# Seven block products for eight in half of the first feed-forward product, with one weight sum of a step made by an adding DMA

## The chip, the cores and the metric

The kernel runs on one core of one Trainium2 chip. The time is device microseconds of one execution. The profile shows the engines PE (matrix products; PEld is its weight load), DVE (vector), ACT (scalar functions), POOL and SP (here the engine that issues most DMAs), and the DMA queues.

## The reference

One layer of a residual block in float32: 256 positions, 2048 channels, a feed-forward width of 8192. Two mixing branches (retention and latent attention) are gated, added and multiplied by w_out; then comes the feed-forward part, which is what the change touches.

```python
    merged = jax.nn.sigmoid(g_ret) * y_ret + jax.nn.sigmoid(g_mla) * y_mla
    return merged @ w_out
...
        h = h + _mixer(u, positions, w_in[l], ret_norm_g[l], w_ret_o[l], q_a_norm_g[l],
                       w_q_b[l], kv_a_norm_g[l], w_kv_b[l], w_mla_o[l], w_out[l])
        z = _rmsnorm(h, norm_mlp_g[l]) @ w_up[l]
        h = h + jnp.square(jax.nn.relu(z)) @ w_down[l]
    return _rmsnorm(h, norm_f_g)
```

w_up is 2048 x 8192 and w_down 8192 x 2048, 64 MB each in float32.

## The kernel before

**Precision.** Every float32 operand x is split in two: a high part `hi`, the value rounded to the PE's reduced 32-bit format by a cast on ACT (L151), and a low part `lo = x - hi`, a subtraction on DVE (L152). A product is then three: hi x hi, lo x hi and hi x lo.

**Weights.** `weights` (L146 to L153) loads a block of 128 x 1024 elements (512 KB) with a DMA from SP's queue (L148) into one of five `raw` buffers, and splits it into one of four `hi` and one of four `lo` buffers. A load waits until the split of five blocks earlier has freed its buffer; a split waits until PE has done with the block four earlier.

**w_out stage.** Its products have the form in which the activation is the stationary operand (128 x 128) and 512 weight columns move (L199, L200, L202). For each of four column blocks, the sums are added to the residual `hn` (L778) and their squares summed (L779). `mlp_turn` transposes a finished block of `hn` by PE products with a unit matrix (L764) and splits it with the norm's gain (L219, L220) into `hT`, which holds the feed-forward input transposed, high and low part side by side. The norm's factor is left out here and put in at the end (`rh2`, squared), which the squared ReLU permits.

**First feed-forward product ("up").** It is done in 64 units of 128 columns of w_up (`t_unit`). Here the weights are stationary. A unit has two weight blocks. In `t_pass1` (L159) sixteen matmuls multiply the high parts of the weights by high and low part of `hT` in one go (512 columns: 256 positions twice); in `t_pass2` (L163) sixteen more multiply the low parts by `hT`'s high part (256 columns). Then `joined` adds the two halves of the accumulator: ACT copies one half out of PSUM (L206) and DVE adds (L207). One DVE operation (L800) squares the ReLU into `hid`, which stays on the chip: 64 tiles of 128 x 256. The first two units are started with the first half of the channels while `mlp_turn(3)` still prepares the last quarter of `hT`.

**Second product ("down").** For each of the 64 tiles of `hid`, ACT and DVE split it (L216, L217) and 24 matmuls (L814 to L816) multiply it with two w_down blocks into eight PSUM accumulators (`dn`), which take all eight banks. After the last tile the residual is added, the final norm computed and the output stored.

**Buffers.** PSUM has eight banks of 128 x 512: four from the pool that `mmps` takes, four from the pool of `atps`. `big` gives out six large SBUF slots of 16 KB per partition, which tensors take in turn as earlier ones die.

**Order.** Each engine works through its own queue in order. The order in a queue is not that of the program text: at build time a scheduler with a simulated timeline places the instructions of the whole program, so weight splits stand well ahead of the matmuls that use them. DMA loads stand in SP's queue, one behind the other; a load whose buffer is not free holds those behind it.

Of the kernel before, what the change touches and what calls it, by code (L numbers as in the profile page):

```python
# [19 lines left out]
P = 128  # L20
# [9 lines left out]
FT = DFF // P  # L30
EPS = 1e-6
# [57 lines left out]
def block_kernel(ctx: ExitStack, tc: tile.TileContext, A):  # L89
# [43 lines left out]
    def mmps(name):  # L133
        return pmm.tile([P, 512], F32, tag="mm", name=name)
# [68 lines left out]

    def join(out, ps):
        t = sm.tile([P, S], F32, tag="join", bufs=2, name="join")
        SC.copy(t, ps[:, S:])  # L206
        V.tensor_tensor(out=out, in0=ps[:, :S], in1=t, op=ALU.add)  # L207
# [25 lines left out]
    cold = cp.tile([P, 512], BF16, name="cold")  # L233
# [5 lines left out]
    rctx = ExitStack()  # L239
    rope_pool = rctx.enter_context(tc.tile_pool(name="rope", bufs=2))  # L240
# [109 lines left out]
    rxb = cp.tile([P, S], F32, name="rxb")  # L350
# [4 lines left out]
    def table(j):  # L355
        ang, kk = angs[j]
        sgn = vec[:, V_INV + 2 + j : V_INV + 3 + j]
        own = ip if j == 0 else cp
        cos = own.tile([P, S], F32, name=f"cos{j}")
        sin = own.tile([P, S], F32, name=f"sin{j}")  # L360
# [158 lines left out]
    with ExitStack() as mctx:  # L519
        cc = big("cc", F32R, shape=(P, 2 * LT, 2, S))  # L520
        kpe = cp.tile([P, S], F32, name="kpe")
# [245 lines left out]
    hp = ctx.enter_context(tc.tile_pool(name="hp", bufs=1))  # L767
    ssh = cp.tile([P, 2, 4], F32, name="ssh")
# [16 lines left out]
    up = [mmps(f"z{i}") for i in range(2)]  # L785
    for i in range(2):
        t_half(up[i], A["w_up"][i], hT, 0)
        if i == 0:
            mlp_turn(3)
    hid = [big(f"hid{i}") for i in range(3)]  # L790
    hid.append(hp.tile([P, KT, S], F32, name="hid3"))
    for i in range(FT):
        if i < 2:
            pz = up[i]
            t_half(pz, A["w_up"][i], hT, 1)
        else:
            pz = mmps(f"z{i}")
            t_unit(pz, A["w_up"][i], hT)
        z = joined(pz)
        V.scalar_tensor_tensor(hid[i // KT][:, i % KT], in0=z, scalar=0.0, in1=z, op0=ALU.max, op1=ALU.mult)  # L800
# [18 lines left out]
    for i in range(FT):  # L819
        dh = hp.tile([P, S], F32R, tag="dh", bufs=3, name=f"dh{i}")  # L820
        dl = hp.tile([P, S], F32R, tag="dl", bufs=3, name=f"dl{i}")
        split(dh, dl, hid[i // KT][:, i % KT])
        ws = []
        for half in range(2):
            w = weights(A["w_down"][i][:, half * 1024 : (half + 1) * 1024], [P, 1024])
            ws.append(w)
            if i < FT - LAST:
                for t in range(2):
                    for c in (2 * half, 2 * half + 1):
                        down(i, t, c, w, (dh, dl))  # L830
        if i >= FT - LAST:
            tail.append((i, ws, (dh, dl)))
# [7 lines left out]
    def finish(t, c, lo, hi, n):  # L840
# [3 lines left out]
        junk = hp.tile([P, 512], F32, tag="junk", bufs=2, name=f"junk{t}{n}")  # L844
# [101 lines left out]
```

## Time and profile before

| | |
|---|---|
| median of 3 runs | 1631.94 us (1631.42 to 1632.12) |
| the profiled execution | 1632.22 us, its span in the profile 1630.4 us |
| PE, DVE, ACT, POOL busy | 1614.9, 996.2, 809.7, 49.5 us |
| granted TensorE clock, mean | 0.998 |
| DMA moved | 304.46 MB, mean 187 GB/s |
| first z matmul, first dn matmul | 915.47 us, 1272.66 us from the span's start |
| weight loads of w_up: 128 of 512 KB | 4.2 us from issue to landing (median) |
| loads of 256 KB (w_mla_o; con) | 2.6 us; 13.4 us |
| stores of 256 KB (out) | 2.5 us |

A group's line in the profile reads: line, engine, operation, output<-inputs, shapes, count | busy us, mean ns of one | idle us of the engine just before, and what ended it. A window's row reads: start:end, length, then busy us and (instructions) of PE, PEld, DVE, ACT and POOL, then the granted PE clock as a share of full speed, the busy share of the DMA engines, and GB/s. A line of the timeline reads: start, duration, engine, line, operation, and how many instructions were run together.

### The profile page before, as it was taken

Reading aid. Unit: us, or ns where it says so; the run is one execution under the profiler, and the core shown is the slowest. Engines: PE = TensorE matmul, PEld = TensorE weight load, DVE = VectorE, ACT = ScalarE, POOL = GpSimd, SP = SyncE. Lnnn points to the kernel's source line nnn. Section 1 sums busy time; section 2 is a strip of 40 time slices with the busy share of each in tenths; the row PEclk is TensorE's granted clock in tenths of the full one; section 3 lists DMA queues with packets and bytes.
Section 4 is the critical chain, followed back from the end, with each engine's and each line's share of the span. In section 5 each row is a group of like instructions: output and inputs, shape, how many; then the busy total and the mean of one; then the engine's idle time right before and its main releaser. Section 6 shows DMA issues by size and latency. Waiting matters only on the chain.

```text
span 1630.4 us, 23041 instructions
## 1 busy us (share of the span) xinstructions
PE 1614.9 (99%) x8782; PEld 1398.8 (86%) x8782; DVE 996.2 (61%) x1491; ACT 809.7 (50%) x1249; POOL 49.5 (3%) x62
## 2 busy tenths in 40 slices
PE   8999999999999999999999999999999999999997
PEld 6888888888889889888888888888888888888886
DVE  7974588655556658666765555555555555555555
ACT  6544555544445556765545544444444444444444
POOL 7100000000000000000000000000000000000001
PEclk9999999999999999999999999999999999999999
DMA  8665544555556554325575555555555655555553
GB/s 306 200 233 193 187 156 166 169 192 186 190 170 203 190 191 146 125 94 176 186 246 187 174 193 188 192 189 186 191 192 184 223 194 192 193 193 195 192 194 112
DMA packets 84480, 304.46 MB, mean 187 GB/s; under 512 B 9360, under 2 KB 9488, under 8 KB 83600
## 3 DMA queue, kind: packets, MB, share of 16 engines
q1 hardware_dynamic: 84368, 302.98, 55.3%
q8 instruction: 69, 1.13, 0.3%
q14 instruction: 43, 0.35, 0.1%
HBM read 300.84 MB, written 2.10 MB: 186 GB/s over the span
## 4 chain that ended last, share of the span: by engine, by line
PE 97%; DVE 1%; issue 0%; DMA 0%; ACT 0%; POOL 0%; SPq 0%; DVEq 0%; POOLq 0%; ACTq 0%
PE z L159 14%; PE z L163 8%; PE dn L816 7%; PE dn L814 7%; PE dn L815 7%; PE rg L159 4%; PE yr L159 4%; PE gr L159 4%; PE gm L159 4%; PE mo L159 4%; PE qk L159 2%; PE gr L163 2%; PE yr L163 2%; PE gm L163 2%; PE rg L163 2%; PE mo L163 2%
## 5 line engine op out<-in xcount | busy, mean ns | idle before, releaser
L152 DVE TENSOR_TENSOR lo<-raw,hi 128x1024 fp32r<-128x1024 f32 (+2 forms) x562 | 666.0, 1204 | 521.6 <-ACT hi L151 248.3
L151 ACT CAST hi<-raw 128x1024 fp32r<-128x1024 f32 (+2 forms) x562 | 580.8, 1035 | 536.9 <-PE z L159 135.2
L159 PE MATMUL z<-hT,hi 128*128 128x512 f32 x1024 | 245.5, 391 | 0.0
L159 PEld LDWEIGHTS z<-hT,hi 128*128 128x128 f32 x1024 | 188.0, 188 | 36.1
L815 PE MATMUL dn<-lo,dh 128*128 128x512 f32 x512 | 199.2, 389 | 0.0
L816 PE MATMUL dn<-hi,dl 128*128 128x512 f32 x512 | 199.2, 389 | 0.0
L814 PE MATMUL dn<-hi,dh 128*128 128x512 f32 x512 | 198.9, 389 | 0.0
L163 PEld LDWEIGHTS z<-hT,lo 128*128 128x128 f32 x1024 | 131.6, 191 | 5.1
L163 PE MATMUL z<-hT,lo 128*128 128x256 f32 x1024 | 133.1, 283 | 0.0
L815 PEld LDWEIGHTS dn<-lo,dh 128*128 128x128 f32 x512 | 96.1, 188 | 20.1
L816 PEld LDWEIGHTS dn<-hi,dl 128*128 128x128 f32 x512 | 96.1, 188 | 19.9
L814 PEld LDWEIGHTS dn<-hi,dh 128*128 128x128 f32 x512 | 96.1, 188 | 19.8
L216 ACT CAST dh<-hid 128x256 fp32r<-128x256 f32 x64 | 26.0, 407 | 89.3 <-PE dn L815 89.3
L159 PE MATMUL mo<-my,hi 128*128 128x512 f32 x256 | 65.5, 396 | 0.4 <-DVE val L207 0.4
L159 PE MATMUL rg<-x,hi 128*128 128x512 f32 x256 | 64.0, 395 | 0.0
L159 PE MATMUL yr<-ry,hi 128*128 128x512 f32 x256 | 61.4, 391 | 0.0
L159 PE MATMUL gr<-x,hi 128*128 128x512 f32 x256 | 61.3, 391 | 0.0
L159 PE MATMUL gm<-x,hi 128*128 128x512 f32 x256 | 61.1, 391 | 0.0
L159 PEld LDWEIGHTS gm<-x,hi 128*128 128x128 f32 x256 | 47.0, 188 | 9.1
L159 PEld LDWEIGHTS gr<-x,hi 128*128 128x128 f32 x256 | 47.0, 188 | 9.0
L159 PEld LDWEIGHTS yr<-ry,hi 128*128 128x128 f32 x256 | 46.9, 188 | 9.0
L159 PEld LDWEIGHTS rg<-x,hi 128*128 128x128 f32 x256 | 46.2, 188 | 8.6
(271 smaller groups left out, 2239.1 us busy)
## 6 DMA issues: line engine op xcount, KB each, us to landing
raw<-w_up SPq DMA_DIRECT2D x128, 512.0 KB, 4.2
raw<-w_down SPq DMA_DIRECT2D x128, 512.0 KB, 4.3
raw<-w_rv SPq DMA_DIRECT2D x32, 512.0 KB, 4.5
raw<-w_rg SPq DMA_DIRECT2D x32, 512.0 KB, 4.5
raw<-w_gret SPq DMA_DIRECT2D x32, 512.0 KB, 4.3
raw<-w_ret_o SPq DMA_DIRECT2D x32, 512.0 KB, 4.6
raw<-w_gmla SPq DMA_DIRECT2D x32, 512.0 KB, 4.4
raw<-w_out SPq DMA_DIRECT2D x32, 512.0 KB, 3.7
```

Source lines behind the costliest of these rows:

```text
L151: SC.copy(hi, raw)
L152: V.tensor_tensor(out=lo, in0=raw, in1=hi.bitcast(F32), op=ALU.subtract)
L159: PE.matmul(out, w[0][:, k], x.both(k0 + k), start=start and k == 0, stop=False)
L163: PE.matmul(out[:, :S], w[1][:, k], x.hi(k0 + k), start=False, stop=stop and k == n - 1)
L216: SC.copy(hi, val)
L814: mm(PE.matmul(out, dh[:, ts], hi[:, ws], start=i == 0, stop=False))
L815: mm(PE.matmul(out, dh[:, ts], lo[:, ws], start=False, stop=False))
L816: mm(PE.matmul(out, dl[:, ts], hi[:, ws], start=False, stop=end))
```

## The change

The first 4096 of w_up's 8192 columns are no longer done in units. They are done by Strassen's scheme in the form with seven products: the operand is seen as 2 x 2 blocks, here 128 positions by 128 channels, the weights as 2 x 2 blocks of 128 channels by 512 columns, and seven products of sums of blocks stand for eight products of blocks.

- **Groups and steps.** Four groups `u` of 1024 columns, each of eight steps `j` of 256 channels. A step (`s_step`) does the seven products of one pair of channel blocks, three matmuls of 512 columns each (hi x hi, lo x hi, hi x lo; L271 to L273), into seven accumulators `qs` that live through the whole group, in seven PSUM banks. The operand sum is now the stationary operand and the weights move.
- **Weight sums.** Of the four 128 x 512 weight blocks of a step two are loaded as `ra`, one as `rb` and one into the buffer `f1`. The first sum is made by a DMA from POOL's queue that adds another block (read from DRAM) onto the one that lies in `f1` (L248). The three others are DVE operations (L253 to L255). There are three `f1` buffers in turn and one `f2`. Then the seven weight operands are split as before, four splits with seven 512-column blocks in total.
- **Operand sums.** `Combos` forms the four sums of `hT`'s blocks that are needed and splits them, in four parts: parts 0 and 1 within the w_out stage (L869), parts 2 and 3 among the early units. They use `raw` buffers as scratch.
- **End of a group.** `s_end` forms the four output blocks from the seven accumulators, with one ACT copy and seven DVE operations of 512 columns. The result lies with the positions in the partitions; `turn` transposes it on PE, 16 transposes in four parts for each group, and `square` works on two 128-column tiles at once. The parts are called in the middle of later steps.
- **Units.** The other 4096 columns stay units; three early ones and two late ones frame the mixture of steps and units.
- **hid.** `square` now computes ReLU and square on ACT, in one buffer `hs`, and stores the result to DRAM from ACT's queue. Down reads it back in 32 loads (`hl`, L963) from SP's queue, and starts with the tiles of the units. `hn` is stored to DRAM too (L920) and read back before the end (L939).
- Some constants of earlier stages move to a pool that is released, and w_up's first half is laid out in steps on the host.

```diff
@@ -28,6 +28,11 @@
 CHUNK = 64
 DFF = 8192
 FT = DFF // P
+SU = 4
+SJ = KT // 2
+ST = SU * 1024 // P
+EARLY, LATE = 3, 2
+SSF = 68
 EPS = 1e-6
 QK_SCALE = float(192.0 ** -0.5)
 LOWEST = -3.4e38
@@ -201,6 +206,88 @@
         for k in range(nk):
             PE.matmul(out, x.hi(k0 + k, ts), w[1][:, k], start=False, stop=stop and k == nk - 1)
 
+    PRODUCTS = ((3, 0, 0), (4, 0, 1), (2, 1, 0), (6, 1, 1), (5, 2, 0), (1, 2, 1), (7, 3, 0))
+    count = [0]
+
+    class Combos:
+        FORM = {2: 0, 5: 1, 6: 2, 4: 3}
+        RAW = {1: (1, 0), 3: (0, 1), 7: (1, 1)}
+
+        def __init__(self, name, pair):
+            self.name, self.pair, self.t = name, pair, []
+
+        def make(self, c):
+            if c % 2 == 0:
+                self.t.append(big(f"{self.name}{c // 2}", F32R, (P, KT // 4, 2, 4, P)))
+            x, q = wtile("raw", [P, 2, 2, 2, P]), wtile("raw", [P, 2, 4, P])
+            hi, lo = self.pair.span(4 * c, 4)
+            xs = x.rearrange("p j k t n -> p (j k) (t n)")
+            V.tensor_tensor(out=xs, in0=hi.bitcast(F32), in1=lo.bitcast(F32), op=ALU.add)
+            a11, a12, a21, a22 = (x[:, :, k, t] for t in range(2) for k in range(2))
+            a2, a5, a6, a4 = (q[:, :, f] for f in range(4))
+            V.tensor_tensor(out=a2, in0=a11, in1=a12, op=ALU.subtract)
+            V.tensor_tensor(out=a5, in0=a11, in1=a21, op=ALU.subtract)
+            V.tensor_tensor(out=a6, in0=a2, in1=a21, op=ALU.subtract)
+            V.tensor_tensor(out=a4, in0=a6, in1=a22, op=ALU.add)
+            o = self.t[-1][:, c % 2 * 2 : c % 2 * 2 + 2]
+            split(o[:, :, 0], o[:, :, 1], q)
+
+        def get(self, f, j):
+            if f in self.RAW:
+                k, t = self.RAW[f]
+                ts = slice(t * P, (t + 1) * P)
+                return self.pair.hi(2 * j + k, ts), self.pair.lo(2 * j + k, ts)
+            o = self.t[j // 4][:, j % 4]
+            return o[:, 0, self.FORM[f]], o[:, 1, self.FORM[f]]
+
+    def s_step(qs, src, x, j, between):
+        uid[0] += 1
+        f1, f2 = forms[:, count[0] % 3], forms[:, 3]
+        count[0] += 1
+        nc.sync.dma_start(f1[:, 0], src[:, 3])
+        G.dma_start(f1[:, 0], src[:, 0], accum_op=ALU.add)
+        ra = zp.tile([P, 2, 512], F32, tag="ra", bufs=3, name=f"ra{uid[0]}")
+        rb = zp.tile([P, 1, 512], F32, tag="rb", bufs=3, name=f"rb{uid[0]}")
+        nc.sync.dma_start(ra, src[:, :2])
+        nc.sync.dma_start(rb, src[:, 2:3])
+        V.tensor_tensor(out=f1[:, 1], in0=f1[:, 0], in1=ra[:, 1], op=ALU.add)
+        V.tensor_tensor(out=f2[:, 0], in0=f1[:, 1], in1=ra[:, 0], op=ALU.subtract)
+        V.tensor_tensor(out=f2[:, 1], in0=f1[:, 1], in1=rb[:, 0], op=ALU.add)
+        ws = []
+        for i, r in enumerate((ra, f1, f2, rb)):
+            if i in (1, 2):
+                hi, lo = (
+                    zp.tile([P, 2, 512], F32R, tag=kind, bufs=4, name=f"{kind}{uid[0]}{i}") for kind in ("shi", "slo")
+                )
+            else:
+                hi, lo = (wtile(kind, [P, r.shape[1], 512]) for kind in ("hi", "lo"))
+            split(hi, lo, r)
+            ws.append((hi, lo))
+        for n, (f, i, o) in enumerate(PRODUCTS):
+            if n == 4:
+                between()
+            (ah, al), (hi, lo) = x.get(f, j), ws[i]
+            first, last = j == 0, j == SJ - 1
+            PE.matmul(qs[f], ah, hi[:, o], start=first, stop=False)
+            PE.matmul(qs[f], al, hi[:, o], start=False, stop=False)
+            PE.matmul(qs[f], ah, lo[:, o], start=False, stop=last)
+
+    def s_end(qs, out, tmp):
+        t3, e, f = (tmp[:, i] for i in range(3))
+        c11, c12, c21, c22 = (out[:, t, c] for t in range(2) for c in range(2))
+
+        def tt(o, a, b, op=ALU.add):
+            V.tensor_tensor(out=o, in0=a, in1=b, op=op)
+
+        SC.copy(t3, qs[3])
+        tt(e, qs[6], t3)
+        tt(f, qs[2], e, ALU.subtract)
+        tt(c21, qs[4], f)
+        tt(c11, qs[5], f)
+        tt(e, e, qs[5], ALU.subtract)
+        tt(c12, qs[1], e)
+        tt(c22, qs[7], t3)
+
     def join(out, ps):
         t = sm.tile([P, S], F32, tag="join", bufs=2, name="join")
         SC.copy(t, ps[:, S:])
...
@@ -774,6 +866,8 @@
             n_unit(pss, A["w_out"][4 * c + kq], mg, 4 * kq, 4, kq == 0, kq == 3)
             if kq == 0 and c:
                 mlp_turn(c - 1)
+        if c in (1, 2):
+            hc.make(c - 1)
         for t in range(2):
             V.tensor_tensor(out=hn[:, t, cs], in0=pss[t], in1=hn[:, t, cs], op=ALU.add)
             SC.activation(pss[t], hn[:, t, cs], AF.Square, accum_out=ssh[:, t, c : c + 1])
@@ -782,25 +876,72 @@
     V.tensor_scalar(rh2, rh2, 1.0 / D, EPS, op0=ALU.mult, op1=ALU.add)
     V.reciprocal(rh2, rh2)
 
-    up = [mmps(f"z{i}") for i in range(2)]
-    for i in range(2):
-        t_half(up[i], A["w_up"][i], hT, 0)
+    hid = [hidd.tile([P, 2, S], F32, name=f"hid{i}") for i in range(FT // 2)]
+    zo = big("zo", shape=(P, 2, 4, 512))
+
+    def square(pair, n, val):
+        t = zp.tile([P, 2, S], F32, tag="hs", bufs=1, name=f"hs{pair}{n}")[:, : val.shape[1]]
+        SC.activation(t, val, AF.Relu)
+        SC.activation(t, t, AF.Square)
+        SC.dma_start(hid[pair][:, n : n + val.shape[1]], t)
+
+    def s_units():
+        turns = []
+        for u in range(SU):
+            qs = {f: (mmps if f in (3, 4, 2, 5) else atps)(f"zs{u}{f}") for f in range(1, 8)}
+            for j in range(SJ):
+                s_step(qs, A["w_up_s"][u, j], hc, j, turns.pop(0) if turns and j else lambda: None)
+                yield
+            s_end(qs, zo[:, 0].rearrange("p (t c) n -> p t c n", t=2), zo[:, 1])
+
+            def turn(u, jj):
+                pT = atps(f"zt{u}{jj}")
+                for j in range(2):
+                    kt = 2 * jj + j
+                    for t in range(2):
+                        o = j * S + t * P
+                        src = zo[:, 0, 2 * t + kt // 4, kt % 4 * P : kt % 4 * P + P]
+                        PE.transpose(pT[:, o : o + P], src, ident)
+                square(4 * u + jj, 0, pT.rearrange("p (j n) -> p j n", j=2))
+
+            turns = [lambda u=u, jj=jj: turn(u, jj) for jj in range(4)]
+        for fn in turns:
+            yield
+            fn()
+
+    forms = None
+    steps = s_units()
+    early = [atps(f"z{i}") for i in range(EARLY)]
+    for i, pz in enumerate(early):
+        t_half(pz, A["w_up"][i], hT, 0)
         if i == 0:
             mlp_turn(3)
-    hid = [big(f"hid{i}") for i in range(3)]
-    hid.append(hp.tile([P, KT, S], F32, name="hid3"))
-    for i in range(FT):
-        if i < 2:
-            pz = up[i]
-            t_half(pz, A["w_up"][i], hT, 1)
-        else:
-            pz = mmps(f"z{i}")
-            t_unit(pz, A["w_up"][i], hT)
-        z = joined(pz)
-        V.scalar_tensor_tensor(hid[i // KT][:, i % KT], in0=z, scalar=0.0, in1=z, op0=ALU.max, op1=ALU.mult)
+            keep = hidd.tile([P, 2, D], F32, name="hnkeep")
+            SC.dma_start(keep, hn)
+            hc.make(2)
+            forms = big("forms", shape=(P, 4, 2, 512))
+    for i, pz in enumerate(early):
+        t_half(pz, A["w_up"][i], hT, 1)
+        square((ST + i) // 2, i % 2, joined(pz).unsqueeze(1))
+        if i == 0:
+            hc.make(3)
+    done = 0
+    for i in range(EARLY, FT - ST):
+        while done < SU * SJ and done * (FT - ST - EARLY - LATE) <= (i - EARLY) * SU * SJ:
+            next(steps)
+            done += 1
+        pz = atps(f"z{i}")
+        t_unit(pz, A["w_up"][i], hT)
+        square((ST + i) // 2, i % 2, joined(pz).unsqueeze(1))
+    for _ in steps:
+        pass
+    hn = big("hn2", shape=(P, 2, D))
+    nc.sync.dma_start(hn, keep)
+    zctx.close()
+    jp = ctx.enter_context(tc.tile_pool(name="jp", bufs=1))
 
     pd = [[(mmps if t == 0 else atps)(f"dn{t}{c}") for c in range(4)] for t in range(2)]
-    ssf = cp.tile([P, 2, 68], F32, name="ssf")
+    ssf = cp.tile([P, 2, SSF], F32, name="ssf")
     rf = cp.tile([P, 2], F32, name="rf")
     LAST = 2
 
@@ -816,20 +957,23 @@
         mm(PE.matmul(out, dl[:, ts], hi[:, ws], start=False, stop=end))
 
     tail = []
-    for i in range(FT):
+    for n, i in enumerate((*range(ST, FT), *range(ST))):
+        if n % 2 == 0:
+            hl = hp.tile([P, 2, S], F32, tag="hl", bufs=3, name=f"hl{i}")
+            nc.sync.dma_start(hl, hid[i // 2])
         dh = hp.tile([P, S], F32R, tag="dh", bufs=3, name=f"dh{i}")
         dl = hp.tile([P, S], F32R, tag="dl", bufs=3, name=f"dl{i}")
-        split(dh, dl, hid[i // KT][:, i % KT])
+        split(dh, dl, hl[:, i % 2])
         ws = []
         for half in range(2):
             w = weights(A["w_down"][i][:, half * 1024 : (half + 1) * 1024], [P, 1024])
             ws.append(w)
-            if i < FT - LAST:
+            if n < FT - LAST:
                 for t in range(2):
                     for c in (2 * half, 2 * half + 1):
-                        down(i, t, c, w, (dh, dl))
-        if i >= FT - LAST:
-            tail.append((i, ws, (dh, dl)))
+                        down(n, t, c, w, (dh, dl))
+        if n >= FT - LAST:
+            tail.append((n, ws, (dh, dl)))
     gf = big("gf", shape=(P, D))
     nc.sync.dma_start(gf, A["norm_f_g"].partition_broadcast(P))
     for t in range(2):
...
@@ -883,6 +1027,13 @@
     k, n = w.shape
     u = w.reshape(k // 512, 4, P, n // 512, 512).transpose(3, 0, 2, 1, 4)
     return np.ascontiguousarray(u.reshape(-1, P, 4, 512))
+
+
+def _s_steps(w):
+    k, n = w.shape
+    b = w.reshape(k // 256, 2, P, n // 1024, 2, 512)
+    q = np.stack([b[:, 0, :, :, 1], b[:, 1, :, :, 0], b[:, 1, :, :, 1], b[:, 0, :, :, 0]], axis=3)
+    return np.ascontiguousarray(q.transpose(2, 0, 1, 3, 4))
 
 
 def _cols(v):
...
```

More of the change, by code (lines that the diff above doesn't have):

```diff
@@ L231, in block_kernel @@
     SC.activation(warm, halfpi, AF.Copy)
[L233 removed]
+    rctx = ExitStack()
+    rope_pool = rctx.enter_context(tc.tile_pool(name="rope", bufs=2))
+    cold = rope_pool.tile([P, 512], BF16, tag="cold", bufs=1, name="cold")
     V.memset(cold, 0.0)
@@ L357, in table @@
         sgn = vec[:, V_INV + 2 + j : V_INV + 3 + j]
-        own = ip if j == 0 else cp
-        cos = own.tile([P, S], F32, name=f"cos{j}")
-        sin = own.tile([P, S], F32, name=f"sin{j}")
+        cos, sin = (
+            (ip if j == 0 else rope_pool).tile([P, S], F32, tag=f"{name}{j}", bufs=1, name=f"{name}{j}")
+            for name in ("cos", "sin")
+        )
         tc.keep_in_program_order(SC.activation(sin, ang, AF.Sin, scale=sgn))
@@ L931 @@
         "w_out": _n_units(np.asarray(w_out)[0]),
-        "w_up": _t_units(np.asarray(w_up)[0]),
+        "w_up_s": _s_steps(np.asarray(w_up)[0][:, : SU * 1024]),
+        "w_up": _t_units(np.asarray(w_up)[0][:, SU * 1024 :]),
         "w_down": np.ascontiguousarray(np.asarray(w_down)[0].reshape(FT, P, D)),
```

14 lines of the change are left out of this document (8 added, 6 removed).

## The prediction

> **What bounds the kernel now.** I read the busy shares first, then the chain that ended last, then the table of one stretch for the feed-forward stages, then the stage's instructions in order of time on PE, and last the groups on DVE and ACT.
>
> ```profile
> PE 1614.9 (99%) x8782; PEld 1398.8 (86%) x8782; DVE 996.2 (61%) x1491; ACT 809.7 (50%) x1249; POOL 49.5 (3%) x62
> ...
> PE 97%; DVE 1%; issue 0%; DMA 0%; ACT 0%; POOL 0%; SPq 0%; DVEq 0%; POOLq 0%; ACTq 0%
> ```
>
> PE is busy 99% of the span and 97% of the ending chain. So every matmul removed is time, as long as PE stays fed, and every us of PE idle is time too.
>
> ```profile
> core 0: us, PE busy (x) PEld busy (x) DVE busy (x) ACT busy (x) POOL busy (x), PEclk, DMA share, GB/s
> 915.00:1272.00 357.00, 357.00 (x2054) 315.26 (x2053) 202.05 (x267) 162.52 (x203) 0.00 (x0) 1.00 0.56 189
> 1300.00:1400.00 100.00, 100.00 (x443) 82.81 (x442) 53.01 (x56) 44.72 (x56) 0.00 (x0) 1.00 0.58 194
> ```
>
> The first row is the first feed-forward product: PE never idle, DVE at 202 of 357 us (57%), ACT 46%, POOL at nothing, DMA 56%. The second row gives a price: 443 matmuls of 512 columns in 100 us, 0.2257 us each.
>
> ```profile
> 944.23 3.82 PE L159 MATMUL z<-hT,hi 128*128 128x512 f32 x16
> 947.88 2.08 PE L163 MATMUL z<-hT,lo 128*128 128x256 f32 x16
> 949.79 3.82 PE L159 MATMUL z<-hT,hi 128*128 128x512 f32 x16
> ```
>
> One unit (128 columns of w_up) takes 949.79 - 944.23 = 5.56 us: sixteen 512-column matmuls from 944.23 to 947.88 (0.228 each), sixteen of 256 in 1.91 (0.119). The first z matmul starts at 915.47, the first dn one at 1272.66: 357.2 us over 64 units, 5.58 each.
>
> ```profile
> L152 DVE TENSOR_TENSOR lo<-raw,hi 128x1024 fp32r<-128x1024 f32 x538 | 648.4, 1225 | 500.5 <-ACT hi L151 231.3 <-PE z L163 145.1 <-PE gr L163 36.1
> L207 DVE TENSOR_TENSOR val<-z,join 128x256 f32<-128x256 f32 x64 | 26.7, 417 | 0.0
> L800 DVE SCALAR_TENSOR_TENSOR hid<-val 128x256 f32<-128x256 f32 x64 | 27.1, 424 | 2.1
> L151 ACT CAST hi<-raw 128x1024 fp32r<-128x1024 f32 x538 | 565.1, 1052 | 513.3 <-PE z L159 135.2 <-PE dn L816 99.2 <-PE rv L200 43.2
> ```
>
> DVE and ACT wait for PE to free the weight buffers: slack today. Rows overlap at their ends. Back to back, a 1024-column subtraction takes 1.14 us of DVE, a 512-column one 0.63, a 256-column one 0.34; the cast takes 0.97 of ACT, 0.6 for 512 columns.
>
> **The change, part by part.** Times t count from the first z matmul.
>
> *PE.* 32 units go: 32 x 5.57 = 178.3 us. In come 32 steps of 7 products x 3 matmuls of 512 columns, 672 in all. The w_out stage, which has this form (12 matmuls, 907.30 to 910.03), gives 0.2267 each: 152.3 us, 4.76 a step. The 64 transposes cost 0.067 to 0.09 each (the ht rows); at 0.08, 5.1 us. Net 178.3 - 152.3 - 5.1 = **20.9 us saved**; with 0.2257 and 0.2285 a matmul and the ends for a transpose, 19 to 22.5.
>
> *DVE and ACT.* A step needs on DVE three weight sums (512 columns, 3 x 0.63) and the low parts (3 x 1.14 + 0.63): 5.94 us against PE's 4.76. A kept unit needs 2 x 1.14 + 0.34 = 2.62 against 5.57, since its squaring (L800) moves to ACT. Five units lie at the ends, so 32 steps and 27 units are mixed: per step DVE 5.94 + 0.84 x 2.62 = 8.1, PE 4.76 + 0.84 x 5.57 = 9.4. Over the stage DVE gets 129.6 + 60.5 + 18 (28 block sums) + 84 (units) + 10 (operand sums) = 302 us of about 350, 86% instead of 57%. A step's ACT work is 3 x 0.97 + 0.6 = 3.5, a unit's 1.94 + 0.37 and a relu and a square of some 0.4 each: less than DVE's. So PE stays the bound on average, with 14% of cover where there was 43%. In the first of the four groups I sum DVE to 78 us and PE to 75: there a wait of DVE on ACT is time. Such waits total 3.8 us of 357 in the trace of before; bounds 0 and 8 (10% of 78): **2.5 us**.
>
> *The start.* PE has three early units (11.7 us) before the first products, with two operand sums behind them on DVE. Following DVE's queue with the periods above, it reaches the first weight sum at t = 10.5 and the first operand cast is ready at 12.3; from there DVE leads and PE is latest, by **3.5 us**, around the fourth unit (27.8 if PE were the bound, 31.3 by DVE); bounds 1 and 6. The two operand sums placed in w_out put some 5 us each on DVE and ACT and hold 2 of 5 raw buffers; DVE has over 1 us free per 2.72 us of PE there: nothing, bounds 0 and 2.
>
> *The adding DMA.* It stands in POOL's queue, empty here before, behind the landing of its f1 load; the sum L253, then everything behind it on DVE and PE, waits for it. No transfer of this kind is in the trace. Nearest are same-size plain loads from SP (256 KB, 2.6 us); the far row is `con`, also 256 KB, 13.4 at the congested kernel start. I take 5, as it also reads its destination. f1 lands at 2.7, so it lands by 8 against 10.5: nothing. At 13.4 it lands at 16.2, 5.7 us late, all of it time. The Trainium skill ("DMA: Bandwidth & Descriptors", Anatomy of one DMA) puts such a GpSimd-issued transfer at 2.0 us plus bytes over 436e3, so an estimate of 2.6 us, without saying what adding costs; by that it is hidden as well. Later three f1 buffers go round: three steps of 9.4, less 6 to 7 of DVE use and 2.6 of load, leave about 19 us.
>
> *SP, ACT queues and traffic.* A step brings 1 MB over SP and POOL, as its unit did. hid is written (8.4 MB, from ACT) and read back, and hn likewise (2 MB each way): 21 MB on 350 us is 60 GB/s beside 189, against 433 seen at 10 to 12 us. Down's hl loads enter SP ahead of their weights and wait on writes long done, except the last. Nothing, bounds 0 and 2.
>
> *PSUM and the single squaring buffer.* Seven accumulators hold seven banks; one bank is left, through which the units and the transposed blocks pass in turn. A unit behind a block waits until ACT has done relu and square (0.6 each) and, for the relu, until the previous block's DMA has left the single buffer (2.5 us, the `out` row). Following the order: 0.8 twice, about 3.6 around the third group, 1.8 at the fourth: **7.1 us**, bounds 3 and 10. The last four blocks chain through the same buffer before down's last banks are free: **1 us**, bounds 0.5 and 4.
>
> *Clock.* Early in the kernel an idle PE was followed by a lower clock:
>
> ```profile
> 8.00:10.00 2.00, 0.00 (x0) 0.00 (x0) 0.00 (x0) 0.25 (x1) 1.71 (x3) 1.00 1.03 426
> 10.00:12.00 2.00, 0.99 (x3) 0.72 (x4) 1.71 (x4) 2.00 (x7) 1.75 (x4) 0.89 1.03 433
> 12.00:14.00 2.00, 2.00 (x8) 1.61 (x7) 2.00 (x5) 2.00 (x6) 1.92 (x3) 0.50 1.02 428
> 14.00:16.00 2.00, 2.00 (x11) 1.82 (x10) 2.00 (x5) 1.76 (x6) 1.83 (x3) 0.76 1.00 420
> ```
>
> That lost 0.2 + 1.0 + 0.5 = 1.7 us once. One or two waits above may reach that length: **1 us**, bounds 0 and 3.4.
>
> *Sum.* -20.9 + 2.5 + 3.5 + 7.1 + 1 + 1 = -5.8 us. The profiled execution of before took 1632.2 us (span 1630.4 and 1.8 around it), 0.3 over the median of 1631.94: 1626.4, and by the median **1626 us**.
>
> **The rivals.**
>
> *B, nearly all kept.* ACT's writes leave faster, the waits cost 4 us in all: 1631.9 - 20.9 + 4 = 1615. For it: each wait above is a sum of modelled steps of which PE's queue can absorb some. Against: PE can't run past a blocked unit.
>
> *C, feeding becomes the bound.* DVE's queue is in order: sums wait for loads, low parts for casts, joins for PE, and ACT's casts stand behind relus that wait for a DMA. From 9.1 us of additional DVE idle in the dense group (12% of 78) the kernel is slower by over 0.2%; at 12 us, 1638. For it: 231 us of DVE's idle today ended on an ACT cast. Against: there DVE is ahead and casts merely follow late loads.
>
> *D, slower by the adding DMA.* If one takes 20 us it lands at 22.8, the start is 12.3 us late, and the ring's 19 us falls short by about 1 us a step for some of the steps: -5.8 + 12.3 + 5 = +11.5, 1643. It decides from 7.8 + 5.8 + 3.3 = 17 us on. For it: DVE is 86% busy just then and `con` took 13.4. Against: there the DMA share was 1.03, here about 0.7. The Trainium skill ("SBUF — State Buffer", Who interferes with whom) says that GpSimd's descriptors starve while DVE runs in a two-port mode, though a tensor_tensor has none; all DVE work here is of that kind, so by that page D is unlikely. No run shows it yet.
>
> *E.* Terms at middling bounds cancel: 1629 to 1635, no difference.
>
> **How the numbers follow.** This kernel's runs spread 0.04%; from no change a measurement can tell about 0.2%, 3.3 us. My case, 1619 to 1628.6, has 0.38; B 0.15; E 0.15; C 0.19; D 0.13. Faster 0.53, same 0.15, slower 0.32. My own case's range is 1619 to 1629. The whole range: 1614 leaves under 0.05 below; above, half of D and the worst of C, about 0.12, lie over 1641. So 1614 to 1641.
>
> **What would show it.** Steps right: 21 matmuls of L271 to L273 in about 4.76 us where they run unbroken; the stage some 351 us instead of 357.2; DVE about 300 us busy in it; the PE idle of the stage some 15 us, in groups z behind ACT's relu (L884) and zs behind DVE's low parts; the adding DMA landing in 3 to 8 us; down's pace unchanged. Wrong: PE idle beyond 24 us, DVE's idle under sums ending on DMA (D) or on ACT (C), or stage PE under 4 us idle (B). What I fear most is a queue of three engines that wait for each other in a circle, which sums of single waits do not see.

## The result, and the profile after

The changed kernel takes 1685.58 us (median of 4, 1680.61 to 1687.62) against 1631.72: 1.0325 times as long, with a 95% interval of 1.0302 to 1.0349. The forecast was 1626. The profiled execution is the shortest of the four, 1680.61 us with a span of 1678.5; the 48.4 us that it lies over the profiled execution of before are what the traces can explain.

The page, busy time of each engine and the shares of the ending chain:

```profile
PE 1618.4 (96%) x8494; PEld 1380.1 (82%) x8494; DVE 1102.6 (66%) x1607; ACT 888.8 (53%) x1385; POOL 77.9 (5%) x94
...
PE 25%; DMA 2%; ACT 1%; DVE 1%; issue 1%; POOL 0%; DVEq 0%; POOLq 0%; ACTq 0%
```

PE has 288 fewer recorded matmuls and is busy 3.5 us longer. The chain's shares add up to 30% only, so it was followed through the last part alone and says nothing of the first product.

The window of the first product (columns: PE, PEld, DVE, ACT and POOL busy, then clock, DMA share, GB/s):

```profile
915.00:1272.00 357.00, 318.38 (x1539) 261.52 (x1539) 275.64 (x337) 209.66 (x291) 28.18 (x32) 0.95 0.73 227
```

Where PE was busy for all of these 357 us it now idles for 39, and its granted clock is 0.95 instead of 1.00. The work itself costs what was forecast; PE in order of time, where nothing interrupts it:

```profile
1032.42 0.39 PE L271 MATMUL zs<-shi,hc 128*128 128x512 f32 x1
...
1036.05 3.79 PE L164 MATMUL z<-hT,hi 128*128 128x512 f32 x16
1039.68 2.08 PE L168 MATMUL z<-hT,lo 128*128 128x256 f32 x16
1041.59 0.40 PE L273 MATMUL zs<-lo,hT 128*128 128x512 f32 x1
```

Sixteen product matmuls lie between the first two lines: 3.63 / 16 = 0.227 us each, 4.76 for a step of 21. A unit takes 1041.59 - 1036.05 = 5.54.

The first z matmul starts at 915.04, the first dn at 1314.56: 399.5 us instead of 357.2. The longest stops of PE in between (in brackets the idle time and what ended it):

```profile
930.47 0.50 PE L271 MATMUL zs<-shi,hc 128*128 128x512 f32 x1 [2.34 <-ACT shi L303]
1068.66 5.35 PE L164 MATMUL z<-hT,hi 128*128 128x512 f32 x16 [3.57 <-ACT hs L884]
1104.63 6.09 PE L164 MATMUL z<-hT,hi 128*128 128x512 f32 x16 [8.38 <-ACT hs L884]
1185.43 1.12 PE L904 MATMUL zt<-con,zo 128*128 128x128 f32 x4 [5.92 <-ACT hs L884]
1189.76 6.18 PE L164 MATMUL z<-hT,hi 128*128 128x512 f32 x16 [3.21 <-ACT hs L884]
1265.44 0.50 PE L271 MATMUL zs<-shi,hc 128*128 128x512 f32 x1 [3.07 <-ACT shi L303]
1281.32 3.92 PE L164 MATMUL z<-hT,hi 128*128 128x512 f32 x16 [3.00 <-ACT hs L884]
```

Twenty stops of 0.2 us or more add up to 41.5. Five of them, 24.1 us, ended with the ReLU of a transposed block (L884); casts and low parts of the weights ended 13.4, joins (L294) 3.4. The durations show a second loss: the sixteen matmuls behind three of the long stops took 5.35 to 6.18 us, where those in the last line took 3.92, since the clock was low. Summed over one-microsecond windows, busy time times the missing share of the clock is 11.6 us.

How the longest stop came about, all engines in order of time:

```profile
1095.61 0.65 PE L904 MATMUL zt<-con,zo 128*128 128x128 f32 x4
1096.67 0.41 ACT L884 ACTIVATE hs<-val 128x256 f32<-128x256 f32 x1
1097.12 0.42 ACT L885 ACTIVATE hs<-hs 128x256 f32<-128x256 f32 x1
1097.57 0.33 ACTq L886 DMA_DIRECT2D hid<-hs  x1
1103.98 0.60 ACT L884 ACTIVATE hs<-zt 128x512 f32<-128x512 f32 x1 [6.45 <-DMA hid<-hs]
1104.63 1.65 PE L164 MATMUL z<-hT,hi 128*128 128x512 f32 x3 [8.38 <-ACT hs L884]
```

PE has transposed a block into the one spare bank. Its ReLU needs the one buffer `hs`, which holds the unit squared just before; that unit's store leaves at 1097.57 and frees the buffer 6.4 us later. Until then the bank is taken and PE's next unit can't start. The DMA rows (KB each, median us from issue to landing):

```profile
ra<-w_up_s SPq DMA_DIRECT2D x32, 512.0 KB, 5.2
forms<-w_up_s SPq DMA_DIRECT2D x32, 256.0 KB, 3.8
forms<-w_up_s POOLq DMA_DIRECT2D x32, 256.0 KB, 5.4
hid<-hs ACTq DMA_DIRECT2D x32, 128.0 KB, 4.6
hid<-hs ACTq DMA_DIRECT2D x16, 256.0 KB, 4.0
```

A store of 128 KB takes 4.6 us, where the store row of before had 2.5 for 256 KB. The adding DMA takes 5.4.

The second product takes 354.6 us instead of 348.3: of the last group's four blocks three are transposed just before it and one within it, and PE waits 4.0 us in it for their ReLUs and 0.5 us for a cast.

### The profile page after: what moved, and what is told of

Its sections match the earlier page's. It is cut to its first block, busy times and chain, and to the rows that moved or that the text cites. A ratio compares the mean times of both kernels' runs of the same rounds, so it can differ in the third digit from the quotient of the medians.

```text
span 1678.5 us, 23010 instructions
## 1 busy us (share of the span) xinstructions
PE 1618.4 (96%) x8494; PEld 1380.1 (82%) x8494; DVE 1102.6 (66%) x1607; ACT 888.8 (53%) x1385; POOL 77.9 (5%) x94
## 5 line engine op out<-in xcount | busy, mean ns | idle before, releaser
L157 DVE TENSOR_TENSOR lo<-raw,hi 128x1024 fp32r<-128x1024 f32 (+2 forms) x498 | 591.0, 1202 | 383.4 <-ACT hi L156 246.3
L156 ACT CAST hi<-raw 128x1024 fp32r<-128x1024 f32 (+2 forms) x498 | 511.8, 1032 | 415.8 <-PE dn L957 95.8
L164 PE MATMUL z<-hT,hi 128*128 128x512 f32 x512 | 133.1, 414 | 22.4 <-ACT hs L884 18.2
L164 PEld LDWEIGHTS z<-hT,hi 128*128 128x128 f32 x512 | 101.7, 202 | 47.0 <-ACT hs L884 19.6
L303 ACT CAST shi<-forms 128x1024 fp32r<-128x1024 f32 x64 | 66.5, 1048 | 36.7 <-DVE forms L253 22.7
L304 DVE TENSOR_TENSOR slo<-forms,shi 128x1024 fp32r<-128x1024 f32 x64 | 77.2, 1219 | 9.7 <-ACT shi L303 9.6
L168 PEld LDWEIGHTS z<-hT,lo 128*128 128x128 f32 x512 | 66.0, 191 | 3.0 <-DVE lo L157 0.3
L168 PE MATMUL z<-hT,lo 128*128 128x256 f32 x512 | 67.2, 283 | 0.0
L248 POOL DMA_DIRECT2D forms<-w_up_s x32 | 28.2, 887 | 698.6 <-DMA forms<-w_up_s 538.9
L304 DVE TENSOR_TENSOR lo<-ra,hi 128x1024 fp32r<-128x1024 f32 x32 | 39.0, 1219 | 25.3 <-PE z L168 25.0
```

The costliest lines, as they stand in the source:

```text
L156: SC.copy(hi, raw)
L157: V.tensor_tensor(out=lo, in0=raw, in1=hi.bitcast(F32), op=ALU.subtract)
L164: PE.matmul(out, w[0][:, k], x.both(k0 + k), start=start and k == 0, stop=False)
L168: PE.matmul(out[:, :S], w[1][:, k], x.hi(k0 + k), start=False, stop=stop and k == n - 1)
L248: G.dma_start(f1[:, 0], src[:, 0], accum_op=ALU.add)
L303: SC.copy(hi, val)
```

## The experiments

Theory one: the chain through the single store buffer and the spare bank, with the lowered clock behind it. Theory two: the feed of weights by DVE and ACT. Theory three: the adding DMA. Each edit also lets the scheduler place the instructions anew, so an experiment can move waits that it was not meant to touch; where the traces show this, it is said. Times are medians, ratios are to the kernel before in the same comparison.

### The store buffer (e1, e4)

```diff
-        t = zp.tile([P, 2, S], F32, tag="hs", bufs=1, name=f"hs{pair}{n}")[:, : val.shape[1]]
+        m = val.shape[1]
+        t = zp.tile([P, m, S], F32, tag=f"hs{m}", bufs=3 - m, name=f"hs{pair}{n}")
```

In e4 the count is 2 for both widths (`bufs=2`), and dh, dl have 2 buffers instead of 3.

> The single squaring buffer hs becomes three: two of 128x256 for the units, one of 128x512 for the transposed blocks (the read-back buffers hl go from 3 to 2 to make room). Theory one, the chain ReLU - store - next ReLU through the one buffer, and the lower PE clock after its waits: PE's idle ended by the ReLU falls from 24 us in the stage to under 6, the stage's PE busy time falls by 10 us or more, total about 1650 (1642 to 1660). Theory two, the weight feed by DVE and ACT is late anyway and the buffer's wait only covers it: other waits of PE grow by as much, 1675 or more. Theory three, the adding DMA: no change, 1680 to 1688.

> As the split of the squaring buffer, but also two buffers for the transposed blocks (dh, dl and hl with two buffers each make room). Theory one: the 7.9 us that PE still waits for the ReLU at the third group falls under 3, with 2 to 3 us of lowered clock behind it: 1660 (1656 to 1665). Theory two (feed): at least 30 us of PE idle and lowered clock stay, ended by casts and low parts of the weights; the total can't fall under 1655 by buffers.

e1 took 1670.97 (1.0242, 1.0220 to 1.0264), e4 1660.14 (1.0173, 1.0157 to 1.0188). e1 missed its 1642 to 1660 and showed why: the block behind another block still waited, 7.91 of the 12.7 us that were left. With two buffers for blocks this goes too. e4, PE in order of time:

```profile
1067.51 3.93 PE L164 MATMUL z<-hT,hi 128*128 128x512 f32 x16 [0.69 <-ACT hs L885]
1094.77 3.90 PE L164 MATMUL z<-hT,hi 128*128 128x512 f32 x16 [1.36 <-ACT hs L885]
```

These are the stops that were 3.57 and 8.38, and the sixteen matmuls behind them run at full clock again. The ReLU's share fell from 24.1 to 4.7 us, the idle from 41.5 to 25.8, and the kernel by 25 us. The clock loss of the first product stayed, 10.6 us instead of 11.6, because other stops still lower the clock. Theory one holds for about half of the loss, with its part on the clock not shown by this run; 28 us over the kernel before stay, and in e4 18 us of the idle end on casts and low parts.

### The adding DMA (e2)

```diff
-        G.dma_start(f1[:, 0], src[:, 0], accum_op=ALU.add)
+        nc.sync.dma_start(f1[:, 1], src[:, 0])
...
+        V.tensor_tensor(out=f1[:, 0], in0=f1[:, 0], in1=f1[:, 1], op=ALU.add)
```

> The adding DMA alone is undone: both blocks are loaded from SP and DVE adds them (32 more operations of 0.63 us, 20 us of DVE). Theory three, the adding DMA holds the steps up: at least 10 us faster, under 1675. Theory one (buffer and clock): no difference beyond 5 us, 1680 to 1690. Theory two (DVE's feed): 5 to 20 us slower, 1690 to 1705.

1687.31 (1.0339, 1.0324 to 1.0355): no gain, theory three falls. The comparison isn't quite clean: the scheduler now put first sums, which wait for their loads, ahead of `hT`'s last splits on DVE, and PE waited 9.7 us for those at the start; without that it would have been some 1678, an estimate that puts the adding DMA at about 8 us. The bound is loose, since the clock loss grew as well, to 17.5 us. The changed kernel's own trace is firmer: DVE's sums waited for the adding DMA twice, 4.4 us together, and PE's idle on casts and low parts of the summed weights is 9.5 of 41.5 us.

### The other half of the change alone (e3)

```diff
-SU = 4
+SU = 0
```

with `Combos`, its calls, `forms` and `zo` left out.

> All 64 units stay, no step of block products; ReLU and square on ACT, hid and hn stored to DRAM and read back as in the changed kernel. If the detour through DRAM and the squaring on ACT cost nothing by themselves (theories one to three): 1632, within 4 us. If they do (traffic, ACT's queue, the single buffer between units): 1640 or more, with PE idle ended by ACT's ReLU.

1632.44 (1.0005, 0.9996 to 1.0015). ReLU and square on ACT and the way of `hid` and `hn` through DRAM cost nothing by themselves, though a single buffer serves all units: there is no transposed block behind a unit, and several banks. The window:

```profile
915.00:1272.00 357.00, 356.60 (x2050) 314.72 (x2049) 176.50 (x203) 206.36 (x329) 0.00 (x0) 1.00 0.69 229
```

PE is full with ACT at 206 us and 229 GB/s, about the numbers of the changed kernel. The loss belongs to the steps of block products and what they take away from the units.

### All four sums on POOL (e5)

```diff
-        G.dma_start(f1[:, 0], src[:, 0], accum_op=ALU.add)
-        V.tensor_tensor(out=f1[:, 1], in0=f1[:, 0], in1=ra[:, 1], op=ALU.add)
+        nc.sync.dma_start(f1[:, 1], src[:, 0])
+        G.tensor_tensor(out=f1[:, 0], in0=f1[:, 0], in1=f1[:, 1], op=ALU.add)
+        G.tensor_tensor(out=f1[:, 1], in0=f1[:, 0], in1=ra[:, 1], op=ALU.add)
```

and the two sums of f2 likewise, on e4.

> The four buffers, and all four weight sums of a step on POOL instead of one adding DMA and three DVE operations. DVE loses 3 x 32 x 0.63 = 60 us of 302; POOL gets 128 x 1.3 = 166 us (from 1.30 us for 512 columns at the kernel's end). Theory two, DVE's load is what makes the feed late: 10 to 20 us faster than the four buffers alone, 1640 to 1650. If latency through the queues counts and not DVE's load, or POOL and DVE slow each other: no gain or slower, 1660 or more.

1693.47 (1.0375, 1.0360 to 1.0390): 33 us slower than e4. A sum took 1.6 to 2.0 us on POOL (1.30 at the kernel's end), four in a row 7.3, and PE's idle doubled to 51 us, 39 of it on casts and low parts. DVE was not relieved either: its subtractions of 1024 columns took 1.5 to 1.7 us instead of 1.22, and over the first product it was busy 320 us, against 300 in e4. So e5 does not test theory two.

### Two groups instead of four, and the spare bank (e6, e9, e10, e11)

e6 is e4 with

```diff
-SU = 4
+SU = 2
```

> The four buffers, and two groups instead of four (2048 columns by block products, 48 units): PE's saving halves to 10.4 us, the steps lie thinner among the units. If waits and clock losses belong to the steps one by one, they halve too: 1632 + (1660 - 1632) / 2 = 1646. If they come from density (theory two: 86% of DVE), they nearly vanish: 1625 to 1635.

1698.94 (1.0411, 1.0393 to 1.0428), slower than with four groups, against both forecasts. The idle is of a new kind; e6, PE in order of time:

```profile
1267.02 3.96 PE L164 MATMUL z<-hT,hi 128*128 128x512 f32 x16 [1.89 <-DVE val L294]
1274.78 3.92 PE L164 MATMUL z<-hT,hi 128*128 128x512 f32 x16 [1.89 <-DVE val L294]
```

With fewer steps, units follow each other directly, and with seven banks held by the accumulators each must wait until the one before has been joined out of the eighth: 13 times, 27.2 us. PE also waited 12.8 us for low parts of the summed weights, and 19.4 us went by lowered clock. e9 leaves a product out to free a bank:

```diff
-    PRODUCTS = (..., (5, 2, 0), (1, 2, 1), (7, 3, 0))
+    PRODUCTS = (..., (5, 2, 0), (1, 2, 1))
...
-        tt(c22, qs[7], t3)
+        tt(c22, qs[4], t3)
```

> As e6 (two groups, four buffers), but the seventh product is left out (its block takes another one's value, so the result is not the reference's): six accumulators, two spare PSUM banks instead of one, and 48 matmuls of 0.227 us (11 us) fewer. If e6's loss is the one spare bank, through which units that follow each other must wait for the join (27 us of idle in e6, 1.9 at a time, and some 15 of lowered clock and refilling): 1640 to 1655. If the spare bank is not the cause, only the 11 us go: about 1688.

1625.53 (0.9966, 0.9954 to 0.9978). That is 73 us below e6, of which the missing matmuls explain 11. PE's idle fell from 47.8 to 9.8 us, that on joins from 27.2 to 2.9, the lowered clock from 19.4 to 3.2. So the single spare bank is a cause on its own, larger than I had expected even here. The 12.8 us on low parts went too; whether they hung on the bank or on the new order of the queues is not shown. e10 and e11 try to have it with all products: the bank in two halves, units in 256 columns without a join.

```diff
-        pz = atps(f"z{i}")
-        t_unit(pz, A["w_up"][i], hT)
-        square((ST + i) // 2, i % 2, joined(pz).unsqueeze(1))
+        pz = spare()
+        u_unit(pz, A["w_up"][i], hT)
+        square((ST + i) // 2, i % 2, pz.unsqueeze(1))
...
+        turned[0] ^= 1
+        return bank[0][:, turned[0] * S : turned[0] * S + S]
```

> As e6 with all seven products, but the spare PSUM bank serves as two halves: a unit adds hi x hi and hi x lo into the same 256 columns (pass one in 32 matmuls of 256 columns at 0.119 instead of 16 of 512 at 0.228, 0.16 us more a unit, 7 us for 43 units, and no join), and the transposed blocks pass in halves of 256 columns through four small squaring buffers. If the one spare bank is the cause of e6's loss: 1631.7 - 10.4 + 7 + 15 (what e9 lost beside its saved matmuls) = 1643 (1636 to 1650). If e9 was fast for another reason: 1685 or more.

> The same halves of the spare bank with four groups. From e4's 1660: 4.6 us more for 29 units, less the 7 us of waits on ReLU and join and some 4 us of clock: 1654 (1648 to 1660); more than that can't come from the bank, since 18 us of e4's idle end on casts and low parts.

e10 took 1674.28 (1.0260, 1.0244 to 1.0275): 25 us faster than e6, not the 56 expected. e11 took 1676.17 (1.0274, 1.0252 to 1.0295), 16 slower than e4. The halves did not become independent: in e10 PE still stopped 18 times, 9.4 us together, for the ReLU of the unit or block before, and the last blocks stopped PE one behind the other at the end. The direction for two groups is confirmed, the size is not, and for four groups the extra matmul time and new stops outweighed the waits saved.

### The clock (e7)

```diff
-                for j in range(2):
+                for j in [0, 1] * {(0, 1): 12, (0, 3): 24, (1, 2): 18, (1, 3): 10, (2, 3): 10}.get((u, jj), 1):
```

> The changed kernel with the transposes of five parts, before which or behind which PE waits for the ReLU, repeated 10 to 24 times (276 more, 22 us of PE work laid into 24 us of idle). Theory one says the lowered clock follows from idleness: the clock stays full at these places and the 7 us lost there go, about 1679. If the clock falls for another reason, or the repeats only delay the ReLU: 1685 or more.

1689.48 (1.0352, 1.0336 to 1.0367), no gain: repeated transposes cost 0.11 us each where I had reckoned 0.08, so the 276 of them laid 30 us into 24 us of idle. What they show is the clock. The first stretch is the changed kernel's longest stop:

```profile
1096.00:1104.00 8.00, 0.26 (x3) 0.02 (x1) 5.02 (x6) 1.52 (x4) 0.00 (x0) 0.69 0.98 284
```

The same place in e7, PE filled with repeats:

```profile
1100.00:1108.00 8.00, 8.00 (x73) 7.88 (x72) 5.71 (x8) 3.77 (x5) 0.37 (x1) 1.00 0.90 207
```

At like DMA load the clock stays at 1.00. Over the first product the clock loss fell from 11.6 to 6.3 us. The low clock follows PE's stops.

### The feed (e8, e12, e13, e14, e15)

e8 leaves out the low parts of the summed weights, on e4:

```diff
-            split(hi, lo, r)
-            ws.append((hi, lo))
+            if i in (1, 2):
+                SC.copy(hi, r)
+                ws.append((hi, hi))
```

> The four buffers of e4, without the low parts of the summed weights: 64 subtractions of 1024 columns (73 of DVE's 302 us) are left out and the third products read the high part in their place, so PE's work is the same and the result is not the reference's. If DVE's load makes the weight feed late (theory two), the 18 us that PE still waits on casts and low parts and most of the 11 us of lowered clock go: 1632 to 1642. If it is the chain from load to sum to cast to PE and not the load, only the 5 us of waits on low parts go: 1652 to 1658.

1662.39 (1.0188, 1.0171 to 1.0205): 73 us of DVE work less, no gain, and outside both ranges. So DVE's load alone isn't the limit. PE's idle on casts rose from 13.1 us in e4 to 21.0, that on the ReLU from 4.7 to 10.0. DVE's waits show what came in its place; the first sum's waits for its loads (us in total, times, longest) in e4:

```profile
DVE forms L253 <- DMA ra<-w_up_s: 38.5, 18, 5.5
```

and in e8:

```profile
DVE forms L253 <- DMA ra<-w_up_s: 95.3, 27, 7.9
```

DVE hurries ahead and then waits for a load that was issued only when a low part had freed its buffer. e12 takes five buffers for `ra` and `rb` instead of three (`bufs=3` to `bufs=5` in both lines).

> As e8 (low parts of the summed weights left out, so the result is not the reference's), and in the room that frees five buffers each for the loaded blocks ra and rb instead of three. The traces show the first sum waiting for an ra load that was issued only when the low part had freed its buffer, and 5 us on the way. If that ring of three is what makes the feed late: e8's 21 us on casts go, with most of the clock loss: 1635 (1630 to 1645). If the high and low buffers that PE frees are the limit: 1655 or more.

1658.83 (1.0170, 1.0155 to 1.0185), a gain of 3.6 us; the wait went to the next ring, f1 with its two loads in a row:

```profile
DVE forms L253 <- DMA forms<-w_up_s: 57.9, 12, 10.9
DVE forms L253 <- DMA ra<-w_up_s: 35.3, 13, 5.6
```

e13 deepens that as well:

```diff
-        f1, f2 = forms[:, count[0] % 3], forms[:, 3]
+        r = count[0] % 5
+        f1, f2 = (forms[:, r] if r < 3 else more[:, r - 3]), forms[:, 3]
```

with four `ra` and four `rb`; e14 is e13 with e2's edit.

> As e12, with the three rings of loads deeper together: five f1 pairs instead of three, four ra and four rb (low parts of the summed weights left out, so the result is not the reference's). If too few load buffers make the feed late (each load is issued only when a low part has freed its buffer, then is 5 us on the way, 10 with the adding DMA): the sums' wait for DMAs falls from 93 us of DVE to under 30 and PE's idle on casts from 17 to under 6: 1640 (1633 to 1646). Rival, the high and low buffers that PE frees or the order in the queues: 1653 or more.

> As e13, with the first sum made by DVE from two SP loads instead of by the adding DMA. If the rings are the cause, no further difference: within 4 us of e13. If the adding DMA's chain (load, then a second DMA through POOL, 4.0 + 5.6 us) is what is left: 8 us or more faster than e13.

e13 took 1640.85 (1.0060, 1.0045 to 1.0075): 21.5 us below e8, in the range expected of the rings. The detail came out otherwise: DVE still waited 67 us for `ra`, but further ahead of PE, whose idle on casts was 8.7 us instead of 21 in e8. These 12 us, and 3.5 of lowered clock, are what the feed can have gained; PE's idle on the ReLU fell by 6.7 us as well, which load buffers don't explain. e14 took 1663.83 (1.0201, 1.0184 to 1.0218), 23 us slower: without the adding DMA the first sums stood ahead of `hT`'s splits again (7.2 us of idle at the start), idle on low parts was 9.5 us instead of 1.5, and the clock loss 15.3 instead of 6.4. In this order of queues the adding DMA is worth having.

e15 asks for the rings with the whole computation; the room comes from two of the four `slo` buffers.

```diff
-        f1, f2 = forms[:, count[0] % 3], forms[:, 3]
+        r = count[0] % 4
+        f1, f2 = (forms[:, r] if r < 3 else more[:, 0]), forms[:, 3]
...
-        ra = zp.tile([P, 2, 512], F32, tag="ra", bufs=3, name=f"ra{uid[0]}")
+        ra = zp.tile([P, 2, 512], F32, tag="ra", bufs=4, name=f"ra{uid[0]}")
```

> The whole computation, with e4's four squaring buffers, four f1 pairs and four ra buffers instead of three, and two buffers instead of four for the low parts of the summed weights (slo) to make room. If the load rings are the limit with DVE's full work too: the sums' wait on ra falls well below e4's 38 us and the time to 1645 to 1655. If the two slo buffers or DVE's load take their place: 1660 or more, with PE's idle ended by slo.

1660.76 (1.0175, 1.0158 to 1.0192), as e4. The first sums' wait for `ra` fell from 38.5 to 21.1 us, but that for f1 with its adding DMA rose from 4.7 to 36.3, and PE now waited 8.8 us for `slo`. So too few load buffers are shown as a limit of the feed with part of DVE's work left out; that deeper rings would pay with all of it isn't shown, since there was no room for them. No version with the whole computation came near the kernel before, and none is offered: the best, e4, is 1.7% slower.

## Why the prediction was wrong

The step that failed is the part on PSUM and the single squaring buffer, with the clock behind it: 7.1 and 1 us in the sum, 24.1 and 11.6 in the trace. Term by term, against the profiled execution:

| term | forecast, us | measured, us |
|---|---|---|
| PE work saved | -20.9 | about -19 (0.227 a matmul, 5.54 a unit, 0.11 a transpose) |
| ReLU, buffer and bank | +7.1 (3 to 10) | 24.1, and 3.4 on joins |
| start and first group, feed | +6.0 | 8.9 up to 1054 us, 14.0 in all |
| clock | +1 (0 to 3.4) | 11.6 |
| second product | +1 (0.5 to 4) | 6.3, of it 4.0 on ReLUs |
| restarting after a stop | not in the sum | some 5.6 |

**PE's saving** was right within 2 us, and so was that the matmuls keep their price. A part of four transposes sets the products behind it back by 0.45 us: starts lie at 1050.23 and 1050.82, 0.59 apart instead of 0.23, and the next comes 0.09 late. Sixteen parts make 7.2 us, where I had 5.1.

**Buffer and bank.** The places were right: the five stops are the ones that I had walked through. The size was not. I took 2.5 us for the store, from a row at the quiet end of the kernel, and let the chain begin at the previous block; here a store takes 4.0 to 4.6, and 6.4 from issue to release at the longest stop, where the DMA share was 0.98. It starts late: before four of the five stops the unit squared last stands just ahead of the block, before the fifth another block. e1 and e4 confirm it with 15 and 25 us. What I missed wholly is that the bank alone, without any store, stops PE for 1.9 us or more whenever one unit follows another within a group (e6; with a second bank, in e9, at most 1.2).

**Clock.** I had the price of one event right, 1.7 us, and allowed for one or two. There were six lowered stretches, four of 3.41 us, which cost at most 1.7 each at half clock, and two of 10.24 and 13.65, because the stops were more, longer and closer together.

**Restarting.** Between 1052.72 and 1053.54 lie two starts 0.82 us apart, where 0.23 is the rule; 0.42 are counted as idle, and the next start came 0.11 late as well. By this one stop I estimate that each costs 0.28 us more than its idle time shows; twenty make 5.6. Some 3 us of the whole stay unassigned.

**Feed.** I weighed DVE's load (86%) and sized the waits of the feed by it. The load came out as reckoned, 301 us busy against 302, but e8 says that it isn't what makes the feed late. The loads were limited by their buffers: I had checked that the ring of f1 gives 19 us, but not that `ra` is held until its low part is made, which itself waits for PE to free a buffer. My closing fear, of queues that wait for each other in a circle, was the right picture, and I gave it no price. That the start came out at 3.5 us, as forecast, is luck: I had DVE behind with its queue, and the trace has the first sum waiting for the first adding DMA.

**Rivals.** B, waits hidden, and E, no difference, are refuted. C, the feed, was there with 14 us, less than the bank and buffer; its mechanism was another one. D, the adding DMA, is refuted as the cause: 5.4 us against my 5, 4.4 us of DVE's waits in all, and e2 and e14 are not faster. My "hidden" was still wrong at the start: the first one landed at about t = 13.5 instead of 8, and DVE waited 2.8 us for it, in a stretch with a DMA share above 1. The Trainium skill ("DMA: Bandwidth & Descriptors", Anatomy of one DMA) gave 2.6 us for it, half of what was measured. The Trainium skill's rule that GpSimd's descriptors starve while DVE runs in a two-port mode ("SBUF — State Buffer", Who interferes with whom) exempts tensor_tensor, and the trace agrees: 5.4 us with DVE 77% busy, near the 5.2 of `ra` and `rb` from SP.

## What to carry to other kernels

Saving matmuls in a kernel with PE at 99% pays only if the new form leaves PE as much slack in accumulators and buffers as the old one: seven accumulators in eight banks turned every unit and every transposed block into a possible stop, and a stop was paid as idle, as restart and, where PE idled for about half of a 3.41 us slot, as lowered clock too. Price a chain through a single buffer with the DMA time of that stage, not with the row of a quiet one, and look at which release starts it. When an engine that feeds PE seems too busy, first see what it waits for: here taking away a quarter of DVE's work in this stage changed nothing, and more load buffers on top of that cut PE's waits on casts by 12 us.

## What the runs showed of the hardware

The granted clock after stops of PE, changed kernel. All its changes in a run lie on a grid of 3.41 us, so the windows here are slots of this grid:

```profile
1095.63:1099.04 3.41, 0.63 (x5) 0.39 (x4) 3.32 (x3) 1.87 (x4) 0.00 (x0) 1.00 0.87 221
1099.04:1102.45 3.41, 0.00 (x0) 0.00 (x0) 1.38 (x2) 0.00 (x0) 0.00 (x0) 0.50 1.06 290
1105.87:1109.28 3.41, 3.41 (x9) 2.65 (x9) 2.13 (x2) 1.93 (x3) 0.00 (x0) 0.50 0.44 154
...
1262.89:1266.30 3.41, 0.86 (x4) 0.67 (x4) 2.65 (x4) 1.68 (x2) 0.00 (x0) 1.00 0.20 72
1266.30:1269.71 3.41, 3.41 (x9) 2.36 (x8) 3.41 (x4) 1.54 (x3) 0.00 (x0) 0.50 0.48 145
...
1276.54:1279.95 3.41, 1.77 (x10) 1.25 (x8) 2.21 (x2) 2.06 (x4) 0.00 (x0) 1.00 0.12 40
1279.95:1283.37 3.42, 2.05 (x9) 1.72 (x10) 0.15 (x1) 1.23 (x2) 0.00 (x0) 1.00 0.94 283
```

PE stopped at 1096.3; the clock halved 2.8 us later and came back 4.6 us after the restart at 1104.6, so the half clock reaches well into the work behind a stop. What counts is how much of one slot PE idles, and not the length of the stop. The stop of 3.07 us before 1265.44 put 2.55 us of idle into one slot and lowered the clock, after PE had restarted; that of 3.00 before 1281.32 was cut by the end of a slot into 1.6 and 1.4 and did not. Stops of 1.02 and 2.15 us with 0.7 us of work between them fell mostly into one slot and lowered it. In e6 stops of 1.89 us lowered it where they lay whole in one slot (before 1231.27 and 1290.11), and did not where a border cut them (before 1267.02 and 1274.78). Over the first product of the changed kernel and all fifteen experiments, every full-clock slot with 1.85 us of idle or more was followed by half clock, and none with less than 1.4; between these both occur. The Trainium skill ("TensorE: Matmul & The Clock Gate", Part 1) gives about 3.4 us of idleness, and as much of work to recover; the length of the slots agrees, but here about half a slot of idleness was enough.

The second thing I had not expected is the price of POOL's sums beside a working DVE (e5): 1.6 to 2.0 us for 512 columns instead of 1.30 alone, and 1.5 to 1.7 us instead of 1.22 for DVE's own subtractions of 1024 columns.
